# A two-layer attention and recurrence block: gate and up by seven block products, casts on ScalarE, one modulation on TensorE

## The chip, the cores and the metric

One core of one Trainium2 chip runs the whole program. The metric is the device time of one execution in microseconds; the kernel before takes 1844.61 us, the median of three runs (1843.56 to 1845.49). A difference of under about 0.2% (some 4 us) can't be told from no change.

## The reference

Two layers work on 512 tokens (`x`) and 256 context tokens (`ctx`), each 1024 wide, in float32. In each layer:

```
sh_m, sc_m, g_m, sh_f, sc_f, g_f = split(silu(c) @ ada_w + ada_b, 6)
u = (rmsnorm(h) * (1 + sc_m) + sh_m) @ w_in
o = concat(neighborhood attention, latent attention, gated recurrence)
h = h + g_m * (o @ w_out)
f = rmsnorm(h) * (1 + sc_f) + sh_f
h = h + g_f * ((silu(f @ w_gate) * (f @ w_up)) @ w_down)
```

`w_gate` and `w_up` are 1024 x 2816, `w_down` is 2816 x 1024. The first layer runs all 768 tokens (the context with its own modulation), the second gives out the 512 tokens alone. The modulation `silu(c) @ ada_w` has 6144 columns in each layer, for `c` and for `c_ctx`.

## The kernel before, in words

**Layout.** The state lies transposed: 8 tiles of 128 features by 768 (or 512) tokens. Every large product is made from matmuls of type fp32r in three terms: each operand is split into a rounded part `hi` and a rest `lo`, and `lin` (L637 to L645) adds hi*hi, hi*lo and lo*hi for each of the 8 blocks of 128 input features. A product over 768 tokens is two matmuls per term, 512 and 256 columns wide (`segs`); over 512 tokens it is one.

**Weights.** `load_w` (L625 to L632) loads a tile into `wst` by DMA on SP's queue, copies it into `whi` (the rounding cast, `copy`, L524 to L533) and writes the rest into `wlo` by a subtraction (`sub` through `tt`, L535 to L539). There are 2 buffers of `wst` and 3 each of `whi` and `wlo` (L466). The cast may go to DVE (L529), POOL (L531) or ACT (L527).

**FFN.** `ffn` (L1325 to L1356) runs over 22 tiles of 128 hidden columns in four groups of 6, 6, 5 and 5 (`GROUPS`, L31). For each tile it makes the gate product and the up product in PSUM buffers of tag `A` (two of two banks each), then `Silu` on ACT, a product with up on DVE, and a split into a hi and lo pair. At the end of a group `deliver` (L1261 to L1291) multiplies the group's tiles with `w_down` for each of the 8 output tiles and adds the result to `h` on DVE (`stt`, L568 to L571). Ahead of it `norm_mod` (L805 to L814) makes the normalized, modulated and split input from `rstd` (L647 to L678), which sums squares on PE, takes the power -0.5 on POOL, spreads it over a tile by a copy (L674) and transposes that.

**Modulation.** `ada_chunks` (L698 to L729) makes 256 columns at a time: 8 pieces of `ada_w` come through 3 buffers `ast`, DVE adds piece times `c` to an accumulator (one instruction a piece, L570), POOL does the same for `c_ctx` (two instructions, L544 and L537), and PE adds up the partitions with a column of ones. In the first layer's mixer `ada_rest` (L895 to L898) makes columns 2048 to 5119 so; columns 5120 on and those of the second layer follow in the first layer's `ffn` (L1332). `ada_later` (L750 to L762, with `ada_cols`, L733 to L748) can make the same on PE, as float32 matmuls of 32 columns of weights into four column groups; with `ADA_PE = 0` it is not used.

**Order.** No engine's order is written by hand. Each operation goes to `Order.add` with a cost; `Order.place` (L304 to L416) plays a list schedule in which a two-engine operation goes where it ends first, and the result is the order in which each engine gets its instructions. The steps of the mixers are fed to it in the order of `PLAN`, with an offset in rank for each (L58 to L91); `FILL_LATE` and `LOAD_EARLY` (L447) shift the modulation and the weight loads.

## Time and profile before

| what | value |
|---|---|
| median of three runs | 1844.61 us |
| the profiled execution's own time | 1840.35 us |
| its span, first to last instruction | 1838.3 us |
| PE busy | 1773.1 us (96%) |
| DVE, POOL, ACT busy | 1100.5, 725.2, 481.4 us |
| mean granted PE clock | 0.992 |

The trace falls into stretches: the start to 45 us, the first layer's mixer to about 490, its FFN to about 1090, the second layer's mixer to about 1440 and its FFN to the end. PE's records overlap (a matmul's record is longer than the distance to the next), so the time of a matmul in a dense run is read from the starts, not from the mean duration.

### The profile page before, as it was taken

What the parts mean: (1) busy time and instruction counts of PE and PEld (TensorE: products, weight loads), DVE (VectorE), ACT (ScalarE), POOL (GpSimd) and SP (SyncE); (2) the same over time, 40 slices, a digit from 0 to 9 for tenths busy, and PEclk for the clock granted to TensorE, in tenths of its full rate; (3) what the DMA queues carried; (4) which work ended last, traced back from release to release, by engine and by line L of the source; (5) the groups of instructions that cost most, each with busy time, mean ns of one, the idle gap of its engine ahead of it and who ended that gap; (6) DMA issues with size and microseconds to landing.
All of it is one profiled execution on the core that took longest, in us unless ns stands there. A gap on an engine that the chain in (4) does not pass through costs nothing.

```text
span 1838.3 us, 25772 instructions
## 1 busy us (share of the span) xinstructions
PE 1773.1 (96%) x9880; PEld 1411.0 (77%) x9880; DVE 1100.5 (60%) x1850; ACT 481.4 (26%) x912; POOL 725.2 (39%) x698
## 2 busy tenths in 40 slices
PE   8999998899989999999999999999999999999999
PEld 4777765667778888888888887777677878888787
DVE  7765478897576566566634357676876644343443
ACT  4454264663130000000000013654664210000000
POOL 2333467777537766310121022335453122232322
PEclk9999999999999999999999999999999999999999
DMA  8111111224223343444422131111101223323233
GB/s 312 52 53 46 35 50 56 92 93 129 71 94 112 112 125 116 137 153 160 142 78 70 52 109 59 62 53 53 59 24 44 72 89 94 98 86 104 81 99 96
DMA packets 86380, 166.53 MB, mean 91 GB/s; under 512 B 9968, under 2 KB 51312, under 8 KB 86256
## 3 DMA queue, kind: packets, MB, share of 16 engines
q1 hardware_dynamic: 86256, 164.88, 28.3%
q8 instruction: 78, 1.28, 0.3%
q14 instruction: 46, 0.38, 0.1%
HBM read 160.65 MB, written 4.19 MB: 90 GB/s over the span
## 4 chain that ended last, share of the span: by engine, by line
PE 77%; DVE 11%; POOL 3%; issue 3%; DMA 3%; ACT 2%; SPq 0%; DVEq 0%; POOLq 0%; ACTq 0%
PE A L502 62%; PE B L502 10%; PE B L507 4%; DMA ast<-in_ada_dram 2%; DVE acc L570 2%; DVE s L537 1%; POOL rn L670 1%; DVE s L529 1%; DVE wlo L537 1%; POOL acc L537 1%; ACT lo L516 1%; DVE lo L570 1%; DVE whi L529 1%; DVE lo L1300 1%; DVE tmp L537 1%
## 5 line engine op out<-in xcount | busy, mean ns | idle before, releaser
L502 PE MATMUL A<-s,whi 128*128 128x512 f32 (+1 forms) x4340 | 1144.8, 355 | 8.3 <-DVE s L537 2.7
L502 PEld LDWEIGHTS A<-s,whi 128*128 128x128 f32 x4340 | 759.8, 189 | 160.4 <-issue 16.6
L502 PE MATMUL A<-s,wlo 128*128 128x512 f32 (+1 forms) x2138 | 735.7, 354 | 0.1
L502 PEld LDWEIGHTS A<-s,wlo 128*128 128x128 f32 x2138 | 395.9, 189 | 58.0 <-issue 8.0
L529 DVE CAST whi<-wst 128x1024 fp32r<-128x1024 f32 (+2 forms) x183 | 125.8, 688 | 407.4 <-PE A L502 355.6
L537 POOL TENSOR_TENSOR wlo<-wst,whi 128x640 fp32r<-128x640 f32 (+2 forms) x75 | 143.8, 1917 | 428.4 <-DVE whi L529 365.7
L570 DVE SCALAR_TENSOR_TENSOR acc<-ast,cc,acc 128x256 f32<-128x256 f32 x280 | 177.7, 635 | 99.7 <-DMA ast<-in_ada_dram 96.8
L516 ACT ACTIVATE tmp<-A 128x768 f32<-128x768 f32 (+1 forms) x75 | 55.2, 735 | 535.8 <-PE A L502 530.6
L537 DVE TENSOR_TENSOR wlo<-wst,whi 128x1024 fp32r<-128x1024 f32 (+2 forms) x133 | 164.0, 1233 | 6.9 <-POOL whi L531 1.9
L670 POOL TENSOR_TENSOR rn<-rn,con 128x12 f32<-128x12 f32 (+4 forms) x44 | 84.5, 1921 | 181.1 <-DVE rn L544 174.0
L537 POOL TENSOR_TENSOR acc<-acc,ast 128x256 f32<-128x256 f32 x168 | 139.5, 831 | 9.9
L544 POOL TENSOR_SCALAR ast<-ast,cc 128x256 f32<-128x256 f32 x168 | 108.8, 650 | 73.8 <-DVE acc L570 69.2
L502 PE MATMUL A<-s,s 128*128 128x512 f32 (+1 forms) x508 | 124.4, 353 | 13.8 <-ACT lo L516 9.2
L502 PE MATMUL B<-s,s 128*64 128x256 f32 (+2 forms) x720 | 110.6, 353 | 1.3 <-DVE s L529 1.3
L502 PEld LDWEIGHTS A<-s,s 128*128 128x128 f32 x508 | 81.0, 191 | 38.1 <-ACT lo L516 12.9
L507 PE MATMUL B<-ident,tmp 128*128 128x128 f32 (+1 forms) x480 | 78.9, 278 | 19.5 <-ACT tmp L527 11.1
L502 PE MATMUL B<-s,whi 128*128 128x512 f32 (+1 forms) x364 | 93.4, 344 | 0.0
L507 PEld LDWEIGHTS B<-ident,tmp 128*128 128x128 f32 (+1 forms) x480 | 56.6, 142 | 42.3 <-ACT tmp L527 13.4
L502 PEld LDWEIGHTS B<-s,s 128*64 128x64 f32 (+1 forms) x720 | 59.2, 144 | 28.4 <-issue 13.2
L531 POOL TENSOR_SCALAR s<-tmp 128x512 fp32r<-128x512 f32 (+2 forms) x24 | 29.5, 1229 | 127.0 <-DVE tmp L537 114.0
L527 ACT COPY s<-B 128x384 f32<-128x384 f32 (+2 forms) x149 | 67.5, 472 | 38.7 <-PE B L507 35.4
L531 POOL TENSOR_SCALAR whi<-wst 128x1024 fp32r<-128x1024 f32 (+4 forms) x24 | 25.5, 1064 | 122.0 <-PE A L502 73.9
(171 smaller groups left out, 1760.5 us busy)
## 6 DMA issues: line engine op xcount, KB each, us to landing
ast<-in_ada_dram SPq DMA_DIRECT2D x320, 128.0 KB, 2.1
wst<-in_wg_dram SPq DMA_DIRECT2D x44, 512.0 KB, 3.5
wst<-in_wu_dram SPq DMA_DIRECT2D x44, 512.0 KB, 3.6
wst<-in_win_dram SPq DMA_DIRECT2D x32, 512.0 KB, 3.5
wst<-in_wd_dram SPq DMA_DIRECT2D x32, 384.0 KB, 3.1
wst<-in_wd_dram SPq DMA_DIRECT2D x32, 320.0 KB, 2.9
wst<-in_wout_dram SPq DMA_DIRECT2D x16, 512.0 KB, 3.6
hr<-in_x_dram SPq DMA_DIRECT2D x16, 384.0 KB, 3.8
```

Source lines behind the costliest of these rows:

```text
L502: od.add({"t": c / 2.4}, lambda e: nc.tensor.matmul(ap(out), lhsT=ap(lhsT), rhs=ap(rhs), start=start, stop=stop), [out], [lhsT, rhs], heat ...
L507: od.add({"t": 256 / 2.4}, lambda e: nc.tensor.transpose(ap(out), ap(in_), ap(ident)), [out], [in_, ident])
L516: nc.scalar.activation(ap(out), ap(in_), getattr(AF, func), scale=ap(scale), **kw)
L527: nc.scalar.copy(out=ap(out), in_=ap(in_))
L529: nc.vector.tensor_copy(ap(out), ap(in_))
L531: nc.gpsimd.tensor_scalar(out=ap(out), in0=ap(in_), scalar1=1.0, scalar2=1.0, op0=ALU.mult, op1=ALU.mult)
L537: (nc.vector if e == "v" else nc.gpsimd).tensor_tensor(out=ap(out), in0=ap(a), in1=ap(b), op=op)
L544: (nc.vector if e == "v" else nc.gpsimd).tensor_scalar(out=ap(out), in0=ap(a), scalar1=ap(s1), scalar2=ap(s2), op0=op0, **kw)
L570: lambda e: nc.vector.scalar_tensor_tensor(out=ap(out), in0=ap(a), scalar=ap(s), in1=ap(b), op0=op0, op1=op1),
L670: lambda e: nc.gpsimd.tensor_tensor(out=ap(r[:, :w]), in0=ap(r[:, :w]), in1=ap(C("mhalf", 0, w)), op=ALU.pow),
L1300: lambda e: nc.vector.tensor_tensor_scan(out=ap(out), data0=ap(a), data1=ap(u), initial=ap(init), op0=ALU.mult, op1=ALU.add), [out], refs( ...
```

## The change

`GROUPS` becomes five groups of four tiles and one of two. Gate and up are made for two hidden tiles at once, as a 2 x 2 block product: the input features in two halves, the two hidden tiles, and the tokens in two halves of `H` (384 in the first layer, 256 in the second). `weights` makes sums and differences of the four weight blocks, `operands` those of the input, and seven products of `H` columns take the place of eight; the results are put together by additions from PSUM on DVE. The `hi` casts of the FFN's weights, its `w_down` and its activations go to ACT. `wst`, `whi` and `wlo` get 4 buffers each; activations use `lo` buffers for three units in four. `ADA_PE` becomes 16, so that columns 2048 to 6143 of the first layer's modulation are made by `ada_later` on PE; for the second layer's, `ada_chunks` sums the partitions with the accumulator as weights and one column of ones as the moving operand, and `ffn` issues it in eight portions behind its units. `rstd` with one group transposes the spread vector itself, without the copy. The mixers' `PLAN` is a new order and new offsets in both layers; `out` is delivered in two halves of the tokens; costs in the planner change (a charge of 95 ns for changing between kinds of matmul, a rule that keeps POOL's operations and some of DVE's apart in time, a dearer scan).

```diff
-ADA_PE = 0
-GROUPS = ((0, 6), (6, 6), (12, 5), (17, 5))
+ADA_PE = 16
+GROUPS = ((0, 4), (4, 4), (8, 4), (12, 4), (16, 4), (20, 2))
...
-    lru_start @-26, lru_in 0 @6, lru_in 1 @18, lru_gates 1 @-5, latent_rope @-58, latent_kv @561,
+    latent_kv, near_v 1 @-89, lru_in 1 @412, lru_start @-25, lru_in 0 @143, lru_out 1 @-489, near_q 1 @992,
...
-    near_v 0 @-133, lru_start @-282, latent_kv @-254, lru_out 0 @152, latent_rope @-104, lru_in 1 @-27,
+    near_v 0, lru_start @453, latent_kv @-1238, lru_in 1 @165, lru_in 0 @-523, near_k 0 @-303, lru_gates 0 @-593,
...
+                    if e == "g" or e == "v" and op.both:
+                        a, b = port["v" if e == "g" else "g"]
+                        if a <= st < b:
+                            st = b
                     if op.table is not None and e == "s" and table not in op.table:
                         st_key = st + 1300.0
+                    elif e == "t" and op.shape != shape:
+                        st_key = st + SWITCH
...
+SWITCH = 95.0
-LOAD_EARLY, FILL_LATE = 124, 778
+LOAD_EARLY, FILL_LATE = 124, 300
...
-    BUFS = {"s6": 15, "hr": 9, "lo": 7, "tmp": 5, "wst": 2, "whi": 3, "wlo": 3, "acc": 3, "ast": 3, "ma": 4, "mb": 4,
+    BUFS = {"s6": 15, "hr": 9, "lo": 7, "tmp": 5, "wst": 4, "whi": 4, "wlo": 4, "acc": 3, "ast": 3, "ma": 4, "mb": 4,
...
-        rb = f3()
-        g = rows // groups
-        copy(rb[:, : nt * rows].rearrange("p (t g) -> p t g", g=g), r[:, :w].spread(g), "vs")
+        if groups > 1:
+            rb, g = f3(), rows // groups
+            copy(rb[:, : nt * rows].rearrange("p (t g) -> p t g", g=g), r[:, :w].spread(g), "vs")
...
+            q = ps1()[:, : 2 * nv].rearrange("p (j v) -> p j v", v=nv)
+            for v in range(nv):
+                for j in range(2):
+                    mm(q[:, j, v : v + 1], acc[v][:, j * P : (j + 1) * P], C("ones", 0, 1), True, True, f32=True)
...
+    def operands(h, stats, A, b, n):
+        H = n // 2
...
+        def second():
+            two = [pair() for _ in range(2)]
+            for j in range(4):
+                norm(4 + j, 1)
+                put(("B22",), j, two[j // 2], j % 2 * H, xs[4 + j][:, H:n])
+            left, right = lambda k: xs[k][:, :H], lambda k: xs[k][:, H:n]
+            for j in range(4):
+                norm(j, 1)
+                t = f3()
+                tt(t[:, :H], right(j), left(j), ALU.subtract)
+                tt(t[:, H:n], right(4 + j), t[:, :H], ALU.subtract)
+                put(("T1", "T2"), j, pair(), 0, t[:, :n])
+                tt(left(4 + j), left(4 + j), t[:, H:n], ALU.subtract)
+            for j in range(4):
+                tt(right(4 + j), right(4 + j), right(j), ALU.subtract)
+                put(("T4", "T3"), j, pair(), 0, xs[4 + j][:, :n])
...
+    def weights(src, i):
+        Q = D // 2
+        one, two, sums = (buf("wst", [P, D]) for _ in range(3))
...
+        def cast(names, t):
+            hi, lo = buf("whi", [P, t.n], F32R), buf("wlo", [P, t.n], F32R)
+            split(hi, lo, t, "s")
...
+        def low():
+            dma(two, src[i + 1])
+            tt(sums[:, :Q], two[:, :Q], two[:, Q:], ALU.add)
+            tt(sums[:, Q:], sums[:, :Q], one[:, :Q], ALU.subtract)
+        def high():
+            tt(two[:, :Q], one[:, :Q], two[:, :Q], ALU.subtract)
+            tt(one[:, Q:], one[:, Q:], sums[:, Q:], ALU.subtract)
...
+            {"A1": upper, "low": low, "S12": lambda: cast(("S1", "S2"), sums), "high": high,
+             "S4": lambda: cast(("S4",), one[:, Q:]), "S3A": lambda: cast(("S3", "A22"), two)}[which]()
...
+    PRODUCTS = {"P1": ("A11", "B11"), "P2": ("A12", "B21"), "P3": ("S4", "B22"), "P4": ("A22", "T4"),
+                "P5": ("S1", "T1"), "P6": ("S2", "T2"), "P7": ("S3", "T3")}
+    def product(ps, name, made, ops, H, start):
+        a, x = PRODUCTS[name]
+        wh, wl = made[a]
+        for j in range(4):
+            xh, xl = ops[x, j]
+            c = slice(j * P, (j + 1) * P)
+            for i, (w, y) in enumerate(((wh, xh), (wh, xl), (wl, xh))):
+                mm(ps[:, :H], w[:, c], y, start and j == 0 and i == 0, j == 3 and i == 2, more=not start)
...
+        return hs, deliver(l, hs, fetch, os_, 16, nq, [(None, o, nq // 2) for o in (0, nq // 2)])
...
+            def all(self):
+                for what in ("A1", "low", "S12", "high", "S4", "S3A"):
+                    self.prepare(what)
+                a, b, c, d = (ps()[:, :H] for ps in (ps1, ps1, ps1, ps2))
+                self.run(a, "P1", True)
+                copy(self.u, a, "sv")
+                self.run(b, "P6", True)
+                tt(self.u, self.u, b, ALU.add, "v")
+                self.run(a, "P2", False)
+                self.run(c, "P5", True)
+                tt(self.v, self.u, c, ALU.add, "v")
+                self.run(d, "P7", True)
+                tt(self.v, self.v, d, ALU.add, "v")
+                self.run(c, "P3", False)
+                tt(self.high[:, H:n], self.u, c, ALU.add, "v")
+                self.run(d, "P4", False)
+                self.a, self.d = a, d
...
+            for i in range(h0, h0 + hn, 2):
+                sides = [Side(w) for w in (wg_d, wu_d)]
+                if i:
+                    for s in sides:
+                        s.all()
+                else:
+                    together(sides)
+                acts += activate(*sides)
+                if rest:
+                    later(rest.pop(0), FILL_LATE)
```

The first unit of a layer runs gate and up together (`together`): P1 and P2 of both sides, then P3, P5, P6, P7, P4. `activate` ends the four blocks of each side, applies `Silu`, multiplies and splits.


## Rows read from the trace of the kernel before

**Rows 1.** The page: span and busy time by engine.
```profile
span 1838.3 us, 25772 instructions
...
PE 1773.1 (96%) x9880; PEld 1411.0 (77%) x9880; DVE 1100.5 (60%) x1850; ACT 481.4 (26%) x912; POOL 725.2 (39%) x698
```

**Rows 2.** Busy us by stretch: PE, PEld, DVE, ACT, POOL; clock, DMA.
```profile
45.00:440.00 395.00, 364.66 (x2247) 274.08 (x2247) 285.07 (x541) 203.39 (x407) 224.51 (x228) 0.99 0.21 65
490.00:520.00 30.00, 25.32 (x155) 20.28 (x155) 18.62 (x33) 9.84 (x21) 7.32 (x7) 0.89 0.17 54
520.00:1079.00 559.00, 557.76 (x3152) 471.54 (x3151) 313.32 (x478) 39.22 (x57) 201.32 (x219) 1.00 0.36 112
1090.00:1400.00 310.00, 295.59 (x1839) 229.77 (x1838) 223.31 (x377) 167.08 (x309) 133.01 (x109) 0.98 0.17 54
1440.00:1478.00 38.00, 33.16 (x246) 30.27 (x245) 28.13 (x57) 14.62 (x32) 8.85 (x6) 0.96 0.17 55
1478.00:1832.00 354.00, 353.94 (x1516) 284.12 (x1516) 141.70 (x181) 12.57 (x21) 91.70 (x58) 1.00 0.31 95
```

**Rows 3.** Busy us by stretch, 280 to 440 us, the sum.
```profile
sum 160.00, PE 141.29 PEld 97.89 DVE 141.85 ACT 94.33 POOL 121.84; mean PE 35.32 PEld 24.47 DVE 35.46 ACT 23.58 POOL 30.46
```

**Rows 4.** Timeline of PE, 1430 to 1446 us: start, duration, operation.
```profile
1430.21 0.63 PE L502 MATMUL A<-s,whi 128*128 128x512 f32 x2
...
1435.82 0.63 PE L502 MATMUL A<-s,whi 128*128 128x512 f32 x2
...
1436.52 0.40 PE L502 MATMUL B<-s,whi 128*128 128x256 f32 x2
...
1445.15 0.40 PE L502 MATMUL B<-s,whi 128*128 128x256 f32 x2
```

**Rows 5.** The same view, 1070 to 1072 us (both widths in turn).
```profile
1070.29 0.39 PE L502 MATMUL A<-s,wlo 128*128 128x512 f32 x1
...
1071.34 0.39 PE L502 MATMUL A<-s,wlo 128*128 128x512 f32 x1
```

**Rows 6.** The same view, 610 to 613 us, a call of ada_chunks.
```profile
610.56 0.63 PE L502 MATMUL B<-acc,con 128*32 128x256 f32 x4
611.11 0.50 PE L502 MATMUL A<-s,wlo 128*128 128x512 f32 x1
...
612.15 0.50 PE L502 MATMUL B<-con,acc 128*128 128x4 f32 x4
612.51 0.49 PE L502 MATMUL A<-s,whi 128*128 128x256 f32 x2
```

**Rows 7.** Groups by form, DVE: xcount, busy us, mean ns, idle before.
```profile
L570 DVE SCALAR_TENSOR_TENSOR acc<-ast,cc,acc 128x256 f32<-128x256 f32 x280 | 177.7, 635 | 99.7 <-DMA ast<-in_ada_dram 96.8
L537 DVE TENSOR_TENSOR wlo<-wst,whi 128x1024 fp32r<-128x1024 f32 x115 | 147.9, 1286 | 4.1
L529 DVE CAST whi<-wst 128x1024 fp32r<-128x1024 f32 x115 | 89.4, 777 | 234.8 <-PE A L502 194.3 <-issue 32.2 <-PE B L502 2.7
L570 DVE SCALAR_TENSOR_TENSOR hr<-A,mod,hr 128x512 f32<-128x512 f32 x71 | 52.8, 744 | 8.3 <-PE A L502 8.3
...
L570 DVE SCALAR_TENSOR_TENSOR hr<-A,mod,hr 128x256 f32<-128x256 f32 x34 | 16.1, 473 | 0.0
...
L529 DVE COPY tmp<-rn 128x512 f32<-128x512 f32 x8 | 3.5, 433 | 4.1 <-POOL rn L670 4.0
```

**Rows 8.** The same view, POOL.
```profile
L537 POOL TENSOR_TENSOR acc<-acc,ast 128x256 f32<-128x256 f32 x168 | 139.5, 831 | 9.9
L544 POOL TENSOR_SCALAR ast<-ast,cc 128x256 f32<-128x256 f32 x168 | 108.8, 650 | 73.8 <-DVE acc L570 69.2 <-DVE sm L585 3.0 <-POOL s L537 0.6
L537 POOL TENSOR_TENSOR wlo<-wst,whi 128x1024 fp32r<-128x1024 f32 x21 | 53.5, 2548 | 180.3 <-DVE whi L529 168.9 <-PE A L502 9.7 <-issue 1.4
```

**Rows 9.** The same view, ACT.
```profile
L527 ACT CAST whi<-wst 128x1024 fp32r<-128x1024 f32 x3 | 3.1, 1047 | 0.9 <-DMA wst<-in_wout_dram 0.9
```

**Rows 10.** Groups by form, weight loads of PE.
```profile
L502 PEld LDWEIGHTS B<-s,whi 128*128 128x128 f32 x364 | 62.1, 189 | 8.6 <-issue 1.2
```

More of the change, by code (lines that the diff above doesn't have):

```diff
@@ L531, in go @@
                 nc.gpsimd.tensor_scalar(out=ap(out), in0=ap(in_), scalar1=1.0, scalar2=1.0, op0=ALU.mult, op1=ALU.mult)
-        od.add(costs(out.n, in_.psum, engs, 1.04 if in_.psum else 0.52, 0.835), go, [out], [in_])
+        od.add(costs(out.n, in_.psum, engs, 1.04 if in_.psum else 0.52, 0.835), go, [out], [in_], both=not in_.psum)
     def tt(out, a, b, op, engs="vg"):
@@ L551, in ts @@
             c["g"] += 83 * len(refs(s1, s2))
-        od.add(c, go, [out], refs(a, s1, s2))
+        od.add(c, go, [out], refs(a, s1, s2), both=not a.psum)
     def scale_rows(x, r):
@@ L1257, in fetch, with deliver @@
             return load_w(wout_d[l, ot], D)
[L1259 to L1264 removed]
+        return hs, deliver(l, hs, fetch, os_, 16, nq, [(None, o, nq // 2) for o in (0, nq // 2)])
+    def deliver(l, h, fetch, xs, gate, n, cut):
+        normed_next = cut is not None
+        first, second = cut or parts(n)
         late = []
```

255 lines of the change are left out of this document (164 added, 91 removed).

## The prediction

> **What bounds the kernel now.** I read the page first: PE is busy for 96% of the span, every other engine for 60% or less [rows 1]. That share is an average, so I then cut the span into its stretches [rows 2]. In the two FFN stretches PE is idle for 1.2 of 559 us and 0.1 of 354 us, at the full clock: there the time is the number of matmuls times their distance, and nothing else. In the mixers it is not quite so: PE is idle for 30.3 of 395 us in the first and 14.4 of 310 us in the second, and for 4.7 and 4.8 us at the two starts of an FFN, where the clock also falls (0.89 and 0.96 on average). Most of the first mixer's idle time, 18.7 of 30.3 us, lies between 280 and 440 us, where DVE is busy for 141.9 and POOL for 121.8 of 160 us [rows 3]: there the modulation's accumulations share DVE and POOL with the attention.
>
> The price of a matmul is read from starts. 24 matmuls of 512 columns go from 1430.21 to 1435.82, 234 ns each; 72 of 256 columns from 1436.52 to 1445.15, 120 ns each [rows 4]; three of each take 1.05 us [rows 5], 350 ns a pair, as the two prices together. So the time goes with the columns, with some 6 ns to spare, and 384 columns should take 177 ns (the middle of 120 and 234).
>
> **Seven products.** In the first layer a hidden tile's gate or up takes 24 pairs, 24 x 0.350 = 8.4 us; a unit of two tiles and one side, 16.8 us. After, it is 7 products x 4 blocks x 3 terms = 84 matmuls of 384 columns, 14.87 us. Over 11 units and 2 sides: 22 x (16.80 - 14.87) = -42.5 us. In the second layer 48 x 0.234 = 11.23 us become 84 x 0.120 = 10.08 us: 22 x 1.15 = -25.3 us. All of it is on the path, since PE never waits there: **-67.8 us**. The `w_down` matmuls stay as they are.
>
> **Modulation of the first layer on PE.** 16 calls of `ada_later` add 128 float32 matmuls of 256 columns. Four of these in four column groups, one behind the other, moved the next matmul to 0.55 us after their start [rows 6]. If all 128 come in fours, that is 32 x 0.55 = 17.6 us; if each stands alone among the others and costs as much as four, 70.4 us. `ast` has three buffers, so I take runs of three: 43 x 0.55 = 23.7 us. The last two matmuls of a call took 0.36 us [rows 6], 16 x 0.36 = 5.8 us more. Removed are eight calls of `ada_chunks` at 0.55 + 0.36 = 0.91 us, -7.3 us. For the second layer's modulation the new sums are 64 matmuls of one column; two of four columns took 0.36 us, so 64 x 0.18 = 11.5 us in place of 8 x 0.91 = 7.3: +4.2 us. Together **+26.4 us** on PE (20.3 to 73.1).
>
> Off DVE go 16 x 8 instructions of 635 ns, 81 us, and off POOL 128 x (831 + 650) ns, 190 us [rows 7, 8]; three quarters of both lay in the first mixer. DVE there falls from 285 us to about 224, POOL from 225 to about 82 [rows 2]. That should close most of the stretch in which DVE was full, and the modulation's matmuls, which need only their DMA, fit into what is left of the gaps: I take **-20 us** of the 30.3 idle (0 to -30.3). SP's queue issues as many `ast` transfers as before, but now PE frees their buffers and not DVE and POOL; weight loads queue behind a transfer that waits for its buffer.
>
> **The reorder.** It removes and adds no instruction. In the first mixer it is part of the 20 us; in the second 14.4 us of idle are to be had, and an order that meets other waits may lose as much: -3 us (-14.4 to +14.4). The copy that `rstd` drops took 433 ns at 512 tokens [rows 7]; some five of these lie on a path on which PE waits: -2 us (0 to -4).
>
> **What the seven products load on the others.** For each unit and side 3.5 tiles of 1024 columns are cast and subtracted in place of 2, and four sums of 512 columns are made. The cast on ACT takes 1047 ns [rows 9], 3.7 us a side, and ACT was idle for nearly all of both FFNs [rows 2]. It costs nothing as long as it starts when the buffer comes free. On DVE, subtraction at 1286 ns and half of that for a sum of 512: 3.5 x 1.29 + 4 x 0.64 = 7.1 us, against 2 x (1.29 + 0.78) = 4.1 before [rows 7]; 22 x 3.0 = 66 us more in each layer. The recombination adds some 8 additions a unit, 0.47 us at 256 columns, 0.61 at 384 (between the two adds of [rows 7]): 11 x 8 x 0.61 = 54 and 42 us. Two groups more mean 16 more adds into `h` a layer, 16 x (0.744 + 0.473) = 19.5 and 16 x 0.744 = 11.9 us. DVE would be busy for about 313 + 66 + 54 + 20 = 453 us of some 515 in the first FFN and 142 + 66 + 42 + 12 = 262 of 330 in the second [rows 2], with POOL taking part of it. So PE stays the bound on average, but the cover is thinner. What PE may wait for is the refill of a `whi` and `wlo` buffer: four tiles fill all four buffers, so a side's tile is refilled while the other three are used. Between the last use of one and the first use of its successor lie four products, 48 matmuls: 5.8 us in the second layer, 8.5 in the first. The refill is a cast on ACT (1.05) and a subtraction, 1.29 on DVE or 2.55 on POOL [rows 7, 8]: 2.3 to 3.6 us, and what stands ahead of it in the queues. I give each of the 44 sides 0.27 us, **+12 us** (0 to +88, the upper end being 2 us each).
>
> **The two starts of an FFN.** PE can begin with P1 and P2 when the first half of the tokens is normalized, which covers 48 matmuls, 8.5 or 5.8 us. But `operands` then makes differences and 14 pairs instead of 8 on a DVE that was already the limit there, with two sides of weights beside them. I take +4 us each, **+8 us** (-5 to +20; 9.5 us idle now). At the very end the last group has two tiles only, whose split ends just ahead of `w_down`: +2 us (0 to 3).
>
> **The sum.** -67.8 + 26.4 - 20 - 3 - 2 + 12 + 8 + 2 = -44.4 us. The profiled execution took 1840.35 us, so 1796 us; it stands 4.3 us under the median of the three runs, and I leave the forecast at **1796 us**.
>
> **A rule against the change.** The mean weight load is 189 ns [rows 10], longer than the 120 ns between two matmuls of 256 columns [rows 4]: loads run beside other matmuls here. The Trainium skill, page "TensorE: Matmul & The Clock Gate", section "The mechanism", says that a load overlaps matmuls in flight only when its row group differs; all of these use every row, and the trace does not agree. By that rule the 792 matmuls that the second layer gains would each cost a load of its own.
>
> **Rivals.**
> - *Everything hides.* No refill wait, no longer starts, modulation in fours, all of the first mixer's idle time closed: -12 - 8 - 2 - 6.1 - 10.3 = 38 us less, **1758 us**. For it speaks that all of this is ordered ahead of time; against it the full DVE at the starts. Chance 0.18.
> - *The modulation's matmuls stand alone.* 70.4 in place of 23.7 us: **1843 us**, no change; halfway 1819. The three buffers speak for it; against it the gaps of the first mixer, which would take up part of it. Chance 0.12, a third of which ends within 4 us of now or above.
> - *Refill decides (the other side).* A queue of DVE or POOL that holds a subtraction up for longer than four products makes PE wait in every side. Gain and loss meet when each of the 44 sides waits (44.4 + 12) / 44 = 1.3 us. With 2 us each it is +88 in place of +12, **1872 us**. For it: a subtraction on POOL (2.55 us) behind another plus the cast comes to 6.2 us against 5.8; DVE waits 96.8 us for `ast` with everything else behind it [rows 7]. Against it: POOL and DVE can share the work, and no wait shows today. Chance 0.15.
> - *Loads don't hide.* If a matmul could not follow its predecessor in less than a load, 189 ns, the second layer would take 84 x 22 x 69 ns = 128 us more than I count and the first 84 x 22 x 12 = 22: **1946 us**. The 72 matmuls at 120 ns speak against it; only a longer run of them is new. The rule named above would do this. Chance 0.02.
>
> **Chances and range.** The forecast itself, 1775 to 1820, has 0.52; with the first rival and two thirds of the second, faster by over 0.2% (3.7 us, about what a measurement of this kernel can tell from no change) has 0.78, within it 0.03, and slower, with the third and fourth and 0.02 for the rest of the second and what I don't see, 0.19. The range runs from 1755, just past the first rival, to 1850, past the second; it leaves out the refill case and the loads.
>
> **What would show it.** Right: matmuls of 384 and 256 columns 177 and 120 ns apart; FFN stretches of some 520 and 335 us with PE idle for under 10 us each; the first mixer not longer than before, with DVE under 70%. Wrong: PE waiting for `wlo` or for an addition from PSUM in each side; modulation matmuls one by one among the others; FFN starts with PE idle for over 10 us.

## The result, and the profile after

The changed kernel takes 1869.72 us (median of four runs, 1866.44 to 1871.59) against 1844.09 us for the kernel before: a ratio of 1.0139, 95% interval 1.0118 to 1.016. It is **slower by 1.4%**; 1796 us was forecast, and the range ended at 1850. The profiled execution took 1867.92 us.

The page of the kernel after: span, busy time, and the chain that ended last by engine.

```profile
span 1866.1 us, 28108 instructions
PE 1732.2 (93%) x10616; PEld 1475.6 (79%) x10616; DVE 1283.9 (69%) x2149; ACT 725.1 (39%) x1297; POOL 747.5 (40%) x623
PE 65%; DVE 16%; POOL 6%; issue 5%; DMA 5%; ACT 3%; SPq 0%; DVEq 0%; POOLq 0%; ACTq 0%
```

Against [rows 1], PE is busy for 41 us less, which is just what the products and the modulation summed to in the forecast (-67.8 + 26.4 = -41.4). The span is 27.8 us longer all the same, so PE waits for 134 us in place of 65. DVE works 183 us more, ACT 244.

Where it waits is seen by stage. I cut both spans at three marks: the first normalization of each FFN and of the second mixer (DVE's `hr,affn` and `hr,amix` rows). The stages are first mixer, first FFN, second mixer, second FFN; columns as in [rows 2] (stretch, its length, busy PE, PEld, DVE, ACT, POOL, then the granted clock). Before:

```profile
0.00:512.42 512.42, 472.80 (x2828) 347.73 (x2828) 360.41 (x704) 233.36 (x463) 279.07 (x298) 0.99 0.27 91
512.42:1103.26 590.84, 587.31 (x3311) 495.62 (x3311) 334.67 (x513) 48.89 (x75) 206.19 (x223) 1.00 0.36 112
1103.26:1459.31 356.05, 340.39 (x2107) 266.63 (x2107) 245.53 (x418) 176.79 (x335) 144.40 (x118) 0.99 0.17 53
1459.31:1838.30 378.99, 372.58 (x1634) 301.02 (x1634) 159.89 (x220) 22.36 (x40) 95.59 (x59) 1.00 0.30 92
```

After:

```profile
0.00:532.23 532.23, 493.57 (x3075) 369.33 (x3075) 314.68 (x637) 221.03 (x441) 182.81 (x148) 0.96 0.29 95
532.23:1129.28 597.05, 551.51 (x3056) 512.51 (x3056) 447.36 (x681) 182.38 (x285) 284.35 (x248) 0.97 0.34 107
1129.28:1489.56 360.28, 331.07 (x2107) 268.25 (x2107) 237.29 (x408) 174.01 (x325) 147.88 (x129) 0.97 0.15 47
1489.56:1866.10 376.54, 356.07 (x2378) 325.52 (x2378) 284.55 (x426) 147.71 (x246) 132.43 (x100) 0.99 0.30 93
```

The forecast of a stage is added up from the prediction's terms; the copy's 2 us and the refills' 12 us are halved between the layers here.

| stage | before | after | change | forecast of the change |
|---|---|---|---|---|
| first mixer | 512.4 | 532.2 | +19.8 | 22.2 - 20 - 1 = +1.2 |
| first FFN | 590.8 | 597.1 | +6.2 | -42.5 + 4.2 + 6 + 4 = -28.3 |
| second mixer | 356.1 | 360.3 | +4.2 | -3 - 1 = -4.0 |
| second FFN | 379.0 | 376.5 | -2.4 | -25.3 + 6 + 4 + 2 = -13.3 |
| sum | 1838.3 | 1866.1 | +27.8 | -44.4 |

In the first FFN, PE's busy time falls by 36 us and its idle time rises from 3.5 to 45.5. What it waits for behind the start, from the waits of PE between 590 and 1122 us (engine, line, releaser: us in total, times, longest):

```profile
PE B L517 <- DVE acc L586: 8.8, 7, 2.1
PE A L517 <- DVE tmp L553: 4.5, 5, 1.8
PE A L517 <- ACT s L543: 3.4, 3, 1.6
```

`acc` is the second layer's modulation, `tmp` the additions from PSUM, `s` the splits of the activations. `wlo` does not stand among them. At the two starts (55 us from about the first normalization on), DVE is busy nearly throughout and PE is not:

```profile
530.00:585.00 55.00, 40.28 (x175) 35.96 (x176) 53.00 (x71) 28.81 (x53) 38.29 (x30) 0.81 0.12 39
1485.00:1540.00 55.00, 42.02 (x290) 38.14 (x289) 49.70 (x75) 29.76 (x58) 39.23 (x37) 0.91 0.17 53
```

The same 55 us before hold 52.08 and 51.02 us of PE at 0.94 and 0.97.

**The clock** was in no term of the forecast. Its mean falls from 0.992 to 0.973. At the very start of the program it shows best: PE's timeline of the kernel after from 30 us on (start, duration, operation, idle time ahead of it and what ended it), and the clock around it.

```profile
30.69 0.86 PE L517 MATMUL A<-s,whi 128*128 128x512 f32 x3
34.01 1.86 PE L517 MATMUL A<-s,whi 128*128 128x256 f32 x5 [2.45 <-DVE s L586]
37.91 1.44 PE L517 MATMUL A<-s,wlo 128*128 128x512 f32 x3 [2.04 <-DVE wlo L553]
...
40.43 0.63 PE L517 MATMUL A<-s,wlo 128*128 128x512 f32 x1
40.85 0.63 PE L517 MATMUL A<-s,whi 128*128 128x512 f32 x1
42.53 0.58 PE L517 MATMUL A<-s,whi 128*128 128x256 f32 x1 [1.05 <-DVE s L586]
```

```profile
32.00:40.00 8.00, 3.95 (x11) 3.18 (x12) 8.00 (x16) 2.17 (x4) 3.21 (x3) 0.61 0.97 352
40.00:48.00 8.00, 6.95 (x22) 3.15 (x22) 3.68 (x8) 0.59 (x1) 2.19 (x1) 0.54 0.25 75
```

Between 31.55 and 42.53 us PE stands idle three times, 5.5 us together, and the clock sits at the lower of its two levels for most of 16 us; before, the same stretches held 45 and 43 matmuls at 1.00. It had been low earlier, too: 0.57 from 16 to 24 us, beside waits of 1.09 and 1.64 us that ended at 15.40 and 17.34. At the lower level the matmul after one of 512 columns starts 0.42 us later (40.43 to 40.85) and not 0.234, so a wait that brings the clock down costs more than its length. Added up over all stretches in which the trace has the lower level, before and then after, the time is

```profile
sum 30.72, PE 26.89 PEld 20.33 DVE 24.02 ACT 15.52 POOL 10.78; mean PE 4.48 PEld 3.39 DVE 4.00 ACT 2.59 POOL 1.80
sum 102.38, PE 86.97 PEld 68.00 DVE 70.98 ACT 40.35 POOL 50.22; mean PE 4.83 PEld 3.78 DVE 3.94 ACT 2.24 POOL 2.79
```

PE is busy in 87 us of it in place of 27. By 0.42 and 0.234 us a matmul, an estimate, (87 - 27) x (1 - 0.234 / 0.42) = 27 us of PE's busy time are the clock's.

### The profile page after: what moved, and what is told of

Its sections match the earlier page's. It is cut to its first block, busy times and chain, and to the rows that moved or that the text cites. A ratio compares the mean times of both kernels' runs of the same rounds, so it can differ in the third digit from the quotient of the medians.

```text
span 1866.1 us, 28108 instructions
## 1 busy us (share of the span) xinstructions
PE 1732.2 (93%) x10616; PEld 1475.6 (79%) x10616; DVE 1283.9 (69%) x2149; ACT 725.1 (39%) x1297; POOL 747.5 (40%) x623
## 4 chain that ended last, share of the span: by engine, by line
PE 65%; DVE 16%; POOL 6%; issue 5%; DMA 5%; ACT 3%; SPq 0%; DVEq 0%; POOLq 0%; ACTq 0%
PE A L517 37%; PE B L517 24%; PE B L523 4%; DMA ast<-in_ada_dram 3%; DVE wlo L553 3%; DVE tmp L553 3%; POOL wst L553 2%; DVE s L553 2%; DVE acc L586 1%; DVE wst L553 1%; DVE lo L553 1%; POOL s L553 1%; DVE s L545 1%; POOL rn L695 1%; DMA wst<-in_wg_dram 1%
## 5 line engine op out<-in xcount | busy, mean ns | idle before, releaser
L517 PE MATMUL A<-s,whi 128*128 128x512 f32 (+2 forms) x2192 | 554.1, 344 | 21.3 <-DVE tmp L553 6.2
L517 PE MATMUL B<-s,whi 128*128 128x384 f32 (+2 forms) x2032 | 467.4, 323 | 19.0 <-DVE tmp L553 5.5
L517 PEld LDWEIGHTS A<-s,whi 128*128 128x128 f32 x2192 | 380.2, 192 | 75.5 <-DVE tmp L553 10.5
L543 ACT CAST whi<-wst 128x1024 fp32r<-128x1024 f32 (+2 forms) x278 | 224.4, 818 | 491.5 <-PE A L517 257.3
L517 PEld LDWEIGHTS B<-s,whi 128*128 128x128 f32 x2032 | 347.2, 192 | 33.9 <-DVE tmp L553 8.0
L517 PE MATMUL A<-s,wlo 128*128 128x256 f32 (+2 forms) x1064 | 347.7, 340 | 2.0 <-DVE wlo L553 2.0
L553 DVE TENSOR_TENSOR wlo<-wst,whi 128x1024 fp32r<-128x1024 f32 (+3 forms) x263 | 293.1, 1125 | 30.2 <-ACT whi L543 18.1
L517 PE MATMUL B<-s,wlo 128*128 128x384 f32 (+2 forms) x1016 | 301.9, 319 | 0.6 <-DVE wlo L553 0.6
L517 PE MATMUL A<-lo,whi 128*128 128x512 f32 (+1 forms) x776 | 218.7, 358 | 8.6 <-ACT lo L543 6.1
L517 PEld LDWEIGHTS A<-s,wlo 128*128 128x128 f32 x1064 | 200.2, 193 | 16.3 <-DVE wlo L553 2.3
L586 DVE SCALAR_TENSOR_TENSOR acc<-ast,cc,acc 128x256 f32<-128x256 f32 x168 | 98.4, 586 | 40.8 <-DMA ast<-in_ada_dram 38.7
```

The costliest lines, as they stand in the source:

```text
L517: od.add({"t": c}, lambda e: nc.tensor.matmul(ap(out), lhsT=ap(lhsT), rhs=ap(rhs), start=start, stop=stop, skip_group_check=more), [out], ...
L543: nc.scalar.copy(out=ap(out), in_=ap(in_))
L553: (nc.vector if e == "v" else nc.gpsimd).tensor_tensor(out=ap(out), in0=ap(a), in1=ap(b), op=op)
L586: lambda e: nc.vector.scalar_tensor_tensor(out=ap(out), in0=ap(a), scalar=ap(s), in1=ap(b), op0=op0, op1=op1),
```

## The experiments

All times are device times; stages are cut at the same marks. A ratio is to the kernel before, run beside the experiment; stage times come from one profile a run, and one order's first mixer differed by 5 us between profiles, so a few us of a stage mean nothing. The rank of an operation in the planner depends on the number of operations in the whole program; in the edited kernels that number is held at its old value, so that an edit doesn't reorder the rest by this alone.

### The two halves of the change

**Seven products in both FFNs, the rest of the kernel before** (modulation, orders and planner's prices too).

> Before with the changed FFN alone (seven products, casts on ACT, 4 buffers of each weight tag, out in two halves); mixers, modulation on DVE and POOL and planner costs as before. Theory A (the FFN gives its saving back at its two starts and in waits, and the mixers' part of the change costs some 30 us more on its own): first mixer ends near 509 us as before, each FFN within 10 us of the 592 and 382 us of before, in all 1835 to 1855 us. Theory B (the FFN is what costs): 1865 us or more. Theory C (the FFN gains its 68 us and the mixers eat it): 1790 us or less.

Measured: 1929.13 us, 1.0453 (1.0432 to 1.0475). The stages take 529.3, 638.5, 369.9 and 389.9 us. Between 600 and 680 us PE waits for sums of the first layer's modulation, which stand there in the order:

```profile
PE B L514 <- DVE acc L583: 28.6, 3, 11.5
```

**Everything but the seven products** (FFN of before).

> After with the FFN of before (plain products in groups of 6, 6, 5, 5, normalization as before, out in parts of 512 and 256); mixers, modulation on PE and planner as after. Theory A: the first mixer ends near 530 us, 20 us later than before, the whole takes 1865 to 1880 us. Theory B: 1844 us or less. Theory C: 1890 us or more.

Measured: 1888.63 us, 1.0231 (1.0202 to 1.0259); 533.3, 603.3, 369.6 and 381.2 us. The first mixer is as long as in the changed kernel: its 20 us don't come from the products. Either half alone is slower than both together, so the two can't be added up, and theories that put all of the loss in one half fall. Both are plans of their own, and which part of their loss is the plan's they don't show.

**Modulation back on DVE and POOL** (`ADA_PE = 0`).

> After with ADA_PE = 0: the first layer's modulation on DVE and POOL again (all 16 portions in the mixer), order of the mixers as after. If the modulation's matmuls on PE lengthen the first mixer: it ends at 510 us or earlier, 20 us less in all. If it is the new order: it still ends at 525 us or later, and with DVE loaded again rather later than after.

Measured: 1952.96 us, 1.0578 (1.0552 to 1.0605); the first mixer takes 604.2 us, 72 more. This planned order loses far more with the modulation on DVE and POOL.

**The second layer's sums issued one portion later.**

```diff
-            q = ps1()[:, : 2 * nv] ...
+            if due:
+                total(*due.pop())
+            due.append((l, c, nv, acc))
```

> After with the partition sums of the second layer's modulation issued one portion of 256 columns later (one more acc buffer, one rb buffer less). If PE's waits for acc (10.4 us in the first FFN) and the clock lost behind them cost what they show: 10 to 16 us less in all, waits for acc under 2 us. Rival: PE then waits for the next thing, and the time stays within 4 us of after.

Measured: 1870.94 us, 1.0138 (1.0105 to 1.017), the same as the changed kernel; the first FFN 597.1 us as there. PE's wait for `acc` in it falls from 10.4 to 2.0 us, and waits for `tmp` take its place. Whatever stood in front, the time was gone: a sign, and no more, that the queue behind the waits was full, not that one result was late (the edit also takes one more `acc` buffer and one `rb` buffer less, and a new plan).

### Work left out, with the order kept

To take work out without a new plan, the planner sees each operation with its cost and buffers, and nothing is issued for it:

```diff
+        if self.mute:
+            emit = self.instead or (lambda e: None)
         op.i, op.emit, op.cost, op.table = len(self.ops), emit, cost, table
```

**Without modulation, changed kernel and kernel before.** Muted are `ada_later` and `ada_chunks`, all of the modulation but its first four calls; what is left of it is its bias.

> Left out of the changed kernel: the work of the modulation after the first four calls (loads of ast, the sums and their matmuls, in both layers); a copy of the bias takes the place of its last addition. Every other instruction stands in the order that it had. Three theories for the idle time that PE gained in the two FFN stages (41.4 and 22.3 us, against 4.9 and 8.3 before). Queue: DVE's queue is so full that whatever PE needs of it comes late; then any DVE work taken out returns idle time. Chain: PE waits for the length of one step (an addition from PSUM, an activation) that no other work delays. Refill: a side's weight tiles come late, as the prediction's third rival had it. In this run the first FFN stage (592 us) loses PE's own part of the modulation, some 10 us, in any case. Queue: 25 to 35 us less in all, PE's idle time from 41 to about 15. Chain and refill: 10 us less, idle time still 30 or more. First mixer (530 us): if its lost time is the modulation's 54 us of busy PE and 8 us of waits for ast, it ends at 470 to 480; if the new order loses time by itself, at 490 or later.

> The same left out of the kernel before, in its own order. First mixer (509 us): PE loses 18 us of work, and most of the idle time between 280 and 440 us should close, so it ends at 470 to 480. If the reorder of the first mixer is worth nothing by itself, this run's first mixer is as long as that of the changed kernel without modulation, within 5 us; if the reorder loses, it is shorter by 10 us or more; if the reorder gains, longer by 10 or more. First FFN stage: PE's 13 us of sums go, nothing else, as PE never waits there.

Measured: 1792.75 us (0.9702, 0.9672 to 0.9733) and 1786.21 us (0.9667, 0.9634 to 0.97). The first two stages, changed kernel and then kernel before:

```profile
0.00:497.17 497.17, 441.86 (x2755) 349.02 (x2755) 311.37 (x632) 216.99 (x430) 181.79 (x148) 0.98 0.20 68
497.17:1049.25 552.08, 527.96 (x2928) 496.79 (x2928) 344.40 (x488) 182.18 (x285) 193.45 (x128) 0.98 0.24 70
```

```profile
0.00:483.00 483.00, 450.45 (x2756) 341.28 (x2756) 302.06 (x607) 230.83 (x459) 155.91 (x118) 0.99 0.21 70
483.00:1045.63 562.63, 559.82 (x3191) 486.34 (x3191) 208.48 (x289) 45.15 (x65) 73.02 (x43) 1.00 0.22 65
```

Three things follow. In the first FFN the modulation costs 597.1 - 552.1 = 45 us after and 590.8 - 562.6 = 28 before. Of the 45 us, 23.5 are PE's own busy time (10 were expected) and 21.4 idle time, which falls from 45.5 to 24.1 us: 15 were expected of a queue, 30 or more of chain and refill. So the queue theory holds, with less than it forecast, and 10.4 us of what went were the waits for these very sums. In the first mixer it costs 35.0 us after and 29.4 before, so the move to PE itself loses 6 us. And with no modulation in either, the new order is 14.2 us longer in the first mixer and 363.6 - 357.8 = 5.8 us in the second: the reorder loses.

**Without the differences of the input** (T1 to T4).

> Left out of the changed kernel: the differences T1 to T4 at the two FFN starts and their splits (the products read B11 and B21 in their place); every other instruction as it was. Queue: at the starts DVE is busy for 53 of 55 and 50 of 55 us and PE for 40 and 42; without the differences some 25 us of DVE and POOL work go at each start, and the two starts return 10 to 18 us each, 20 to 36 us in all. Chain: the starts wait for normalization, which stays: under 8 us in all. Refill: under 8 us too, since the weights' load stays.

Measured: 1853.09 us (1.0026, 0.9997 to 1.0055). The two starts:

```profile
530.00:585.00 55.00, 47.52 (x245) 44.63 (x246) 46.01 (x73) 31.83 (x58) 29.10 (x24) 0.94 0.16 51
1485.00:1540.00 55.00, 47.71 (x355) 44.22 (x352) 44.98 (x77) 30.70 (x60) 28.76 (x30) 0.94 0.24 73
```

PE works 7 and 6 us more in them, at a higher clock, and the median is 17 us below the changed kernel's (21 by the two ratios): at the low end of the 20 to 36 of the queue theory or under it, twice what the others gave. The six runs lie between 1847.3 and 1861.3 us, so this is rough.

**Without the sums of the weights** (S1 to S4).

> Left out of the changed kernel: the sums S1 to S4 of the weights and the casts and subtractions of S1, S2 and S4 (the products read A11 and A12 in their place); every other instruction as it was. For each side DVE and POOL lose some 4.5 us, ACT 1.5. Queue: the idle time after the starts (26 us in the first FFN, 9 in the second) falls to under 10 in all, and the starts return some 10 us too: 25 to 40 us less. Refill: about the same total, but then the run without modulation returns nothing beyond PE's own part, and the gaps that go are those that name whi or wlo. Chain: less than 10 us.

Measured: 1822.49 us (0.9863, 0.981 to 0.9917); 559.7 and 367.0 us for the FFNs, 47 us less together, more than any theory gave. The edit takes refills away as well as sums, so it doesn't tell queue from refill by itself. But the run without modulation returned idle time too, and the waits of PE that name `wlo` or `whi` come to 3.5 us in the whole span of the changed kernel: this is the queue and not the refill.

**Products alone:** modulation, differences and sums all muted.

> Left out of the changed kernel, all three at once: the modulation after the first four calls, the differences T1 to T4, and the sums S1 to S4 with their casts (the products read blocks that exist); every other instruction in its order. What is left in the FFN stages is the seven products with their additions from PSUM. If the saving was priced rightly and all that went missing in the FFN went to DVE's queue, the first FFN stage takes what it takes before without modulation less the saving, 562.6 - 42.5 = 520 us (515 to 526), the second 379.3 - 25.3 = 354 us (350 to 358). If the products themselves cost more than 84 matmuls at 177 and 120 ns, or the additions from PSUM hold PE up by their length, 535 us or more and 362 or more.

Measured: 1762.09 us (0.9545, 0.9522 to 0.9567).

```profile
504.42:1037.92 533.50, 520.31 (x2928) 491.77 (x2928) 245.75 (x396) 145.00 (x240) 101.04 (x77) 0.99 0.24 70
1397.16:1757.90 360.74, 349.18 (x2378) 321.94 (x2378) 198.94 (x331) 112.61 (x200) 50.86 (x52) 0.99 0.32 94
```

Both lie between the two expectations. PE's busy time falls by 559.8 - 520.3 = 39.5 and 372.9 - 349.2 = 23.7 us against the kernel before without modulation, where 42.5 and 25.3 were forecast; of the stage times 29.1 and 18.6 us are gained. So the price of a product was right; 10 and 5 us are waits that the seven products bring with them (the largest in the first FFN, 4.9 us, is for `rn`, the power on POOL, ahead of its transposes; in the second, 4.8 us in six waits for the last split on ACT at a group's end). The sums and differences then take back 552.1 - 533.5 = 18.6 and 376.7 - 360.7 = 16.0 us.

Side by side, the muted runs show what none shows alone. The first FFN from 55 us behind its first normalization on, in the changed kernel, without modulation, without the sums of the weights, and without both (and the differences):

```profile
587.00:1129.00 542.00, 509.84 (x2875) 474.99 (x2874) 394.22 (x613) 153.05 (x232) 248.14 (x219) 0.99 0.36 114
552.00:1049.00 497.00, 485.99 (x2754) 458.70 (x2752) 292.47 (x423) 152.78 (x232) 157.06 (x99) 1.00 0.25 74
585.00:1090.00 505.00, 492.75 (x2834) 464.30 (x2832) 309.24 (x535) 117.76 (x188) 162.98 (x178) 1.00 0.40 121
559.00:1038.00 479.00, 468.76 (x2660) 442.07 (x2658) 208.70 (x338) 115.37 (x184) 81.10 (x58) 1.00 0.25 75
```

PE's idle time is 32.2, 11.0, 12.3 and 10.2 us. Behind the start, the sums alone cost 0.8 us of it, the modulation alone 2.0, both together 22: the loss is that of two kinds of work in one queue, and it can't be shared out between them.

**Half of the sums of the second layer's modulation from DVE to POOL**, order kept.

```diff
+                    elif v == 0 and nv == 1 and kt > 3:
+                        def go(e, a=acc[v], t=st, w=w):
+                            nc.gpsimd.tensor_scalar(out=ap(t), in0=ap(t), scalar1=ap(w), scalar2=1.0, ...)
+                            nc.gpsimd.tensor_tensor(out=ap(a), in0=ap(a), in1=ap(t), op=ALU.add)
```

> The changed kernel, every instruction in its order, but half of the sums of the second layer's one-vector portions (kt 4 to 7, 64 instructions of 635 ns) done by POOL in two instructions each (650 and 831 ns): 41 us off DVE, 95 us onto POOL, both in the first FFN. If DVE's queue is what PE waits for there, the first FFN shortens by 8 to 20 us (from 597). If POOL's own in-order queue then holds up weight subtractions and products that PE needs, no gain or a loss of up to 15.

Measured: 1899.45 us (1.0278, 1.0259 to 1.0297), the first FFN 625.8 us, 29 us longer. In the groups of PE, the sums of modulation now wait for POOL:

```profile
L517 PE MATMUL B<-con,acc 128*128 128x1 f32 x128 | 19.4, 239 | 22.1 <-POOL acc L739 14.9 <-DVE acc L586 5.6 <-POOL acc L553 1.6
```

DVE is relieved by 25 us and it doesn't help: PE's idle time in the stage goes from 45.5 to 60.8 us, and its clock there from 0.97 to 0.95. The sums are now late from POOL, and PE waits for them all the same.

### Orders

**12 calls of `ada_later` in the kernel before**, and **the new order of the first mixer in the kernel before**.

> The kernel before, with 12 calls of ada_later in place of the six calls of ada_chunks in the first mixer, nothing else edited; the planner places them. From the runs without modulation a call of ada_later costs 35.0/16 = 2.2 us, and a call of ada_chunks 2.8 us of PE and a share of 12 us of idle time. If the move to PE is good in itself: 12 x 2.2 - 29 = 3 us off the first mixer, 505 to 512 us. If it loses (loads of ast that PE waits for, and a clock that falls behind such waits), 520 us or more.

> The kernel before, with the changed kernel's order of the first mixer, nothing else. If the order loses by itself what the runs without modulation say (14 us), the first mixer takes 520 to 535 us, above all in the first 60 us, where PE's gaps and a halved clock would show again. If the order is bad only together with modulation on DVE and POOL, 570 us or more (604 were measured with the new planner's prices). If the 14 us belong to the planner's new prices and not to the order, 505 to 515 us.

Measured: 1888.54 us (1.0230, 1.0209 to 1.025) and 1883.49 us (1.0202, 1.0182 to 1.0223). First mixers:

```profile
0.00:543.79 543.79, 509.06 (x2996) 360.50 (x2996) 306.33 (x624) 225.44 (x447) 170.94 (x136) 0.98 0.27 85
0.00:550.65 550.65, 488.74 (x2828) 360.59 (x2828) 369.79 (x716) 230.61 (x452) 279.01 (x298) 0.96 0.26 84
```

Both lose; the first as its second expectation had it, the second between its first two. The first has 36 us more of busy PE. Its timeline shows one reason: a modulation matmul (a float32 matmul leaves two records) keeps the next one waiting for as long as two of them do.

```profile
396.42 0.62 PE L502 MATMUL B<-ast,cv 128*32 128x256 f32 x2
396.97 0.55 PE L507 MATMUL B<-ident,lo 128*128 128x128 f32 x3
...
398.86 0.62 PE L502 MATMUL B<-ast,cv 128*32 128x256 f32 x4
399.41 0.33 PE L507 MATMUL B<-ident,lo 128*128 128x128 f32 x1
```

The second shows that the new order loses 38 us with the old modulation, more than the 14 that it loses without, and not in the first 60 us, where the clock stays at 1.00. It does so under the old planner's prices, so the new prices are not needed for the loss.

**The old order of the second mixer in the changed kernel.**

> The changed kernel with the order of the second mixer of the kernel before. If the new order of the second mixer is what lost 4 us there, with PE's idle time at 29 us against 16, it takes 354 to 358 us in place of 360, and the rest stays within 3 us a stage. If an order only fits the program that it was searched for, the second mixer takes 365 us or more.

Measured: 1898.64 us (1.0274, 1.0232 to 1.0315; two runs, 1890.71 and 1906.57); the second mixer takes 387.7 us. The old list under the new prices is worse there by 27 us, as the second expectation had it: it did not carry over to another program.

**Seven products in the second FFN alone.**

> The kernel before, with the seven products in the second layer's FFN alone; modulation, both mixers' orders and the first FFN as before. If stages add up, it is the kernel before with 376.5 in place of 379.0 us in the second FFN: 1836 to 1845 us, no difference that counts. If a change at one place shifts the planned order of the rest (the planner weighs the whole program at once), the mixers move by 10 us or more either way, and the total with them.

Measured: 1893.02 us (1.0254, 1.0237 to 1.0272); 533.9, 598.4, 367.0 and 391.4 us. An edit in the last quarter of the program moved the first mixer by 21 us: the planner may use four weight buffers from the start, and plans another order there.

**Seven products in both FFNs, first mixer's order kept:** the planner gets the extra buffers late, so that all ahead keeps its order.

```diff
+    for t, n in (("wst", 2), ("whi", 3), ("wlo", 3)):
+        od.tags[t].free = [0.0] * n + [420000.0] * (4 - n)
     od.place()
```

> The run with the seven products in both FFNs and the rest of the kernel before (1929 us), but with the extra weight buffers only late in the plan (from 420 us of its time), so that the first mixer keeps the order of before. First mixer 510 to 515 us in place of 529. If the 638 us of its first FFN came from the portions of the first layer's modulation that stand there (PE idle for 30 us in front of their sums), they stay at 620 or more; if they came from the disturbed order ahead of it, 600 or less.

Measured: 1908.49 us (1.0327, 1.0308 to 1.0346); the first mixer is back at 500.1 us, the first FFN takes 643.4, so its loss didn't come from the order ahead of it. PE is idle for 76.0 us of it, and 33.8 of these are waits for `acc`, the sums of modulation that stand there.

### Is there a version that gains?

**The second FFN alone, order kept ahead of it** (as above, from 1200 us of the plan), and then **with the new planner's prices in that FFN and its weight casts on ACT**.

> As the run with the seven products in the second FFN alone, but the planner gets the extra buffers of wst, whi and wlo (4, 4, 4 in place of 2, 3, 3) only late in its plan (from 1200 us of its own time), so that both mixers and the first FFN keep the order of the kernel before. If the planned order was what moved the mixers there (first mixer 533.9 us against 512.4), they return to 510 to 515, 589 to 593 and 354 to 360 us, and with a second FFN of 370 to 380 in place of 379 the total is 1832 to 1846. If the buffers or the products themselves slow the rest, it stays above 1865.

> As the run with the seven products in the second FFN alone and the order kept ahead of it (1843.9 us, second FFN 393 us from its first normalization, PE idle for 28 us of it), but the planner uses the changed kernel's prices (matmul by its columns, the wait of DVE and POOL for each other) for the instructions of the second FFN, and all of its weight casts go to ACT. If the planner's prices are why that FFN is 17 us longer than the changed kernel's (376.5 us), it falls to 375 to 384 and the total to 1826 to 1837 us. If it is longer for another reason (the last matmuls of the mixer run after its first normalization there), it stays at 388 or more and the total at 1840 to 1846.

Measured: 1843.92 us (0.998, 0.9971 to 0.9989) and 1837.31 us (0.9953, 0.994 to 0.9966). The second is the first version that beats both kernels, but its stages (507.7, 588.6, 353.8, 386.4 us) don't look like the products' doing: the stages ahead of them are shorter, the FFN itself isn't. It brings four weight buffers where the kernel before has 2, 3 and 3. So the last run is the control, **the kernel before with the four buffers alone**, its plan and the order of every instruction untouched.

> The kernel before with four buffers each of wst, whi and wlo in the program but its own plan, which knows of 2, 3 and 3; the order of every instruction is that of before, and no seven products. The run before this one was 0.5 per cent faster than the kernel before, but its profile has the first mixer 4.7 us and the first FFN 2 us shorter and the second mixer and FFN together 5 us longer. If the gain is the buffers', this kernel gains as much: 1835 to 1841 us, with a first mixer of 500 to 509 us. If it is the seven products', this kernel stays within 2 us of the kernel before.

Measured: 1837.73 us, 0.9953 (0.9936 to 0.9969). The whole gain is the buffers'; the seven products in the second FFN are worth nothing that can be measured, and under the old prices (0.998) they take some of the buffers' gain back. The first mixer may hold most of the 7 us: with the same instructions in the same order it takes 505.9, 507.7 and 508.0 us in the three runs with four buffers, and 512.4 in the one profile without. As one order differs by 5 us between profiles, that is not shown.

## Why the prediction was wrong

- **Seven products, -67.8 us: the price right, the place wrong.** In the kernel after, matmuls of 384 columns follow each other in 177 ns (12 from 709.44 to 711.56), those of 256 in 119 (15 from 1600.09 to 1601.88):

```profile
709.44 0.52 PE L517 MATMUL B<-s,whi 128*128 128x384 f32 x2
...
711.56 0.52 PE L517 MATMUL B<-s,whi 128*128 128x384 f32 x2
...
1600.09 0.40 PE L517 MATMUL B<-s,whi 128*128 128x256 f32 x2
...
1601.88 0.28 PE L517 MATMUL B<-s,whi 128*128 128x256 f32 x1
```

  The step that failed is "All of it is on the path, since PE never waits there": that was read from a kernel with less work on DVE and ACT. With products alone, 47.7 of 67.8 us reach the stages; in the changed kernel without modulation, 10.5 + 2.6.
- **"So PE stays the bound on average, but the cover is thinner": this is where the FFN's time went.** DVE's load was forecast almost right (453 and 262 us; 447 and 285 measured), but it was set against PE as a share of a stretch, and the share doesn't tell. What PE needs next (an addition from PSUM, an operand at the start, a sum of modulation) stands in DVE's queue behind other work. Ahead of 915.30 us it is two subtractions and an accumulation of the modulation; the first three rows are DVE's, the last is PE's:

```profile
911.02 2.35 DVE L553 TENSOR_TENSOR wlo<-wst,whi 128x1024 fp32r<-128x1024 f32 x2
913.29 1.49 DVE L586 SCALAR_TENSOR_TENSOR acc<-ast,cc,acc 128x256 f32<-128x256 f32 x1
914.70 0.54 DVE L553 TENSOR_TENSOR tmp<-tmp,A 128x384 f32<-128x384 f32 x1
915.30 0.62 PE L517 MATMUL A<-s,whi 128*128 128x384 f32 x2 [1.77 <-DVE tmp L553]
```

  The group that answers to [rows 7]:

```profile
L553 DVE TENSOR_TENSOR wlo<-wst,whi 128x1024 fp32r<-128x1024 f32 x165 | 214.1, 1311 | 6.6 <-POOL whi L547 1.9 <-ACT whi L543 1.8
```

  That DVE is busy for 75% of both FFN stages is not the cause by itself. Behind its start the second FFN has as busy a DVE (74%) as the first (73%), and PE waits there for 4.7 us in 294 in place of 32.2 in 542:

```profile
1541.00:1835.00 294.00, 289.32 (x1940) 264.87 (x1939) 218.86 (x326) 109.71 (x173) 86.93 (x56) 1.00 0.32 99
```

  What the first FFN has besides is the modulation, whose accumulations wait on DVE for their transfers for 38.7 us between 590 and 1122 us, with everything else behind them; the prediction saw such waits (96.8 us before) in its third rival alone. Whether these waits or the accumulations' own time did it was not separated. At the starts DVE is full (53.0 and 49.7 of 55 us). Sums and differences cost 35 us with the modulation out, and not the 20 of refills and starts. The Trainium skill, page "TensorE: Matmul & The Clock Gate", section "Architectural detail: the array is 16× 32×32, not 1× 128×128", calls the queues of ACT and DVE strictly first in, first out. No run here tests that rule by itself; the rows at 915 us fit it.
- **Refill waits, +12 us: wrong mechanism.** PE waits for `wlo` for 2.6 us in the whole span, 2.0 of them ahead of 38 us. The rival that refill decides gave 1872 us, near the measured time, but by waits that the trace does not have.
- **Starts, +8 us: too small.** PE's idle time in the 55 us of a start rose by 11.8 and 9.0 us, to 14.7 and 13.0 (a sign of being wrong that the prediction had named), and the clock fell to 0.81 and 0.91 besides.
- **The clock: in no term.** An estimate puts it at 27 us of PE's busy time; it is part of the costs above and below, since it fell in stretches with such waits, and no run separates it.
- **Modulation, +26.4 us: two terms mis-sized.** The four records of [rows 6] at 610.56 us are two matmuls and not four, as a float32 matmul leaves two; a call of `ada_chunks` has eight such records and then four. Muted, ten such calls gave the first FFN of the kernel before 28.2 us, 2.8 each and not 0.91. And the 128 matmuls on PE came in 69 runs, not 43, with 42.5 us to the next matmul in all and not 23.7; the rival in which each stands alone (70.4) held in part. In the first mixer both errors nearly cancel (+6); in the first FFN, where the same accumulations met a DVE with less room, the modulation costs 17 us more than before instead of 4.2, and all of that is idle time (21.4 us of it against 0.7 before; PE's busy time for it fell).
- **First mixer's idle time, -20 us: right by itself, and taken back by the order. Reorder, -3 us: the wrong way.** DVE fell to 59% of the stage and POOL to 34%, and yet PE's idle time went from 39.6 to 38.7 us only. The muted runs take this apart. In the kernel before, the modulation makes the idle time longer, 32.5 to 39.6 us; in the changed kernel its matmuls fill gaps, 55.3 to 38.7. That is -23.7 us where -20 was forecast. But without modulation the new order has 55.3 us of idle time against 32.5. Between 280 and 440 us, where the gaps were to close, they did (18.7 us [rows 3] to 6.0); ahead of 280 us the idle time went from 17.2 to 28.2. In all, 7.9 us of it are waits for `ast`:

```profile
280.00:440.00 160.00, 154.01 (x1102) 105.63 (x1099) 108.97 (x255) 87.46 (x226) 68.52 (x69) 1.00 0.34 103
L517 PE MATMUL B<-ast,cv 128*32 128x256 f32 x256 | 45.1, 395 | 8.7 <-DMA ast<-in_ada_dram 7.9 <-DVE tmp L586 0.5
```

  By the stage times the new order costs some 14 us in the first mixer (muted, it took 497.2 and 504.4 us in two profiles, so some 7 of them are uncertain) and 5.8 in the second. A gain of 3 us, with as much as 14.4 either way, was forecast for the second and none apart for the first: this miss is as large as that of the products.
- **The rule against the change** did not hold here: the mean load is 192 ns in the kernel after, and 119 ns lie between two matmuls.

```profile
L517 PEld LDWEIGHTS B<-s,whi 128*128 128x128 f32 x2032 | 347.2, 192 | 33.9 <-DVE tmp L553 8.0
```

From the kernel before, by the muted runs: products alone -29.1 - 18.6; sums and differences +18.6 + 16.0; modulation +5.6 + 16.8; orders +14.2 + 5.8. That is some 29 us, against 27.8 measured. The shares of sums and modulation hold for this sequence alone: with the modulation in place, leaving out the weights' sums returned 37.4 us of the first FFN. Why the new order loses in the mixers stays open. It loses without modulation too, and the first mixer's new list loses under the old prices (38 us); the old list under the new prices was run for the second mixer alone, where it lost 27 us.

## What to carry to other kernels

When an edit takes work from the bound and gives it to the engines that feed it, the question is not whether they have time on average but what stands in their queue ahead of the instruction that the bound waits for. With DVE busy for 73 and 74%, PE waited for 32 us in one FFN and for 5 in the other; what the first had besides was the modulation, work that itself waits for transfers with the rest of the queue behind it. To price such work, leave it out with every other instruction in its place, singly and together: two works in one queue cost 22 us of waiting, and each alone 2 or less. Runs with halves of the change only mixed the parts with a new order. And give a gain its control: the best version here owed everything to more weight buffers.

## What the runs showed of the hardware

- Three gaps of PE of 1.05 to 2.45 us between 31.55 and 42.53 us came with a granted clock of 0.61 and 0.54 in the 16 us from 32 us on. Over the span the clock's mean fell by 0.019: some 36 us of full-clock time (1866.1 x 0.027 - 1838.3 x 0.008), the idle stretches counted in.
- A float32 matmul of 32 columns of weights and 256 moving columns moved the next matmul by 0.55 us, alone or with another of its kind beside it in another column group (396.42 to 396.97 and 398.86 to 399.41 us).
- One order of instructions doesn't give one time for a stage: the changed kernel's first mixer took 527.0 to 532.3 us in six profiles with the same 3075 PE records.
